# Dilated queries, keys and gates as pairs of 7 block products instead of direct matmuls woven with the attention

## The chip, the cores and the metric

The kernel runs on one core of a Trainium2 chip. TensorE (PE) multiplies, VectorE (DVE), ScalarE (ACT) and GpSimd (POOL) do the elementwise work, SyncE (SP) issues most DMAs and ACT some. Each engine takes its instructions from a queue of its own in order; semaphores between engines make one wait for another. The metric is device microseconds of one execution, median of the runs.

## The reference

The reference is one encoder block over 1024 tokens of width 1024, float32, with three token mixers side by side. Cut to what matters here:

```python
h = rms_norm(x, g_pre)
a_qkv, bq, bk, bv, mq, ga, gb, gm, mg = split(h @ w_in)
aq, ak = rope(a_qkv[:, :, 0], pos), rope(a_qkv[:, :, 1], pos)   # 3 dilations x 8 heads x 64
for gi, (window, dil) in enumerate(((128, 1), (512, 4), (2048, 16))):
    o_g, lse_g = dilated_window_attention(aq[gi], ak[gi], av[gi], window, dil)
oa = sum(softmax(lse over the dilations) * o_g)                 # "combine"
ob, om = grouped_query_attention(...), memory_attention(...)
ya = (oa * silu(ga)) @ w_br_a                                   # likewise yb, ym: "branch products"
merged = sum(sigmoid(mg + b_merge)[i] * (ya, yb, ym)[i])        # 3 x 1024 merge gates
out = x + rms_norm(merged @ w_out, g_post)
```

## The kernel before

All activations are kept transposed, channels in partitions and 1024 tokens along the row. To keep float32 accuracy every operand is split into a high and a low part (`split`, L104: ACT copies the high part, DVE subtracts it, L105/L106), and a product takes three matmuls: high by high, high by low, low by high. `hh[k]`, `hl[k]` are the parts of the normalised input, eight blocks of 128 channels. A *unit* is 128 output channels for all tokens: 8 blocks x 3 matmuls x 2 halves of 512 tokens = 48 matmuls of 512 columns (`dense`, L143, L145, L147).

The stages in order are: norm and loads; memory attention; grouped-query attention; the values of the dilated attention; the dilated attention; the merge gates; the branch products; the output projection.

The values and the merge gates are computed in pairs of units by a scheme of seven block products: a pair is a 2 x 2 block matrix (weights halved along channels, tokens halved), the sums of blocks are prepared beforehand (weight sums `sf` on POOL, L1430, and their splits `ch`; sums of token blocks T1 to T4, stored in memory `tsd` early in the kernel), and seven products of 12 matmuls take the place of eight: 84 matmuls, not 96. Sums of the products give the outputs. Before, each product of a gate pair has a PSUM bank of its own, and DVE rebuilds the outputs (L1453, tiles `v`, `y`, `w`; ACT copies the first product into `p1`, L1467).

The dilated attention has 12 items (4 pairs of heads x 3 dilations). An item needs its query unit and key unit, both turned by rope from PSUM (`rope_half`: four DVE multiplications of 32 partitions and one of 128, L1044/L1045, then a POOL addition, L1051), and then for 8 tiles T of 128 queries: scores on PE (`scores`, L1118), a masked reduction on DVE (`soft`, L1130), exponentials on ACT with their sum (L1133 to L1138; where the two heads' window has to be turned about, in two instructions), transpositions of the probabilities on PE into one of two PSUM banks (`trans`, L1155/L1164), ACT's copy of them out (`app`, L1167), the product with the values (`pv`, L1181), and the sums turned by a transposition (`stats`, L1200). `combine` weighs the three dilations of a pair of heads through a round trip to memory.

The order of PE is written out: `weave` (L174) takes pieces of attention and matmuls of the dense units by turns, by a table of costs, so that matmuls stand between the attention's pieces. 28 units are woven into the attention (24 query and key units, 4 gate units, `add_a`, `add_gate`), two items ahead of the item that reads them. After them come eleven pairs for 22 merge gates (`prod`, `evac`, `slot`), with the last `combine` spread among them; then 24 branch products (`y_unit`, 24 matmuls each, L125, with `y_evac`), then the output. In the value, gate and branch stages the order of ACT, DVE, POOL and SP is written out too; in the attention a scheduler sets it.

```python
                if T == 7:
                    out.append(joined(it["pv"][0], nxt and nxt["scores"][0]))
```
is how a piece of one item and one of the next are put together in the plan of pieces.

## Time and profile before

| | us |
|---|---|
| median of three runs (1447.92 to 1448.38) | 1448.18 |
| span of the profiled execution | 1446.0 |
| PE busy | 1418.7 |
| values, on PE until | 580.35 |
| dilated attention with 28 units, until | 1008.0 |
| eleven gate pairs, until | 1222.07 |
| branch products, until | 1352.63 |
| output projection and end | 93.4 |

Times in rows are microseconds from the start of the span unless a column says ns. A group's row gives line, engine, operation, what it writes and reads, shapes and count, then its busy time, the mean ns of one, and the idle time of the engine just before. Matmuls overlap in the pipeline, so the mean of one is longer than the step from one to the next; the step is read from the chain. The granted TensorE clock was 1.000 over the span.

### The profile page before, as it was taken

Reading aid. Unit: us, or ns where it says so; the run is one execution under the profiler, and the core shown is the slowest. Engines: PE = TensorE matmul, PEld = TensorE weight load, DVE = VectorE, ACT = ScalarE, POOL = GpSimd, SP = SyncE. Lnnn points to the kernel's source line nnn. Section 1 sums busy time; section 2 is a strip of 40 time slices with the busy share of each in tenths; the row PEclk is TensorE's granted clock in tenths of the full one; section 3 lists DMA queues with packets and bytes.
Section 4 is the critical chain, followed back from the end, with each engine's and each line's share of the span. In section 5 each row is a group of like instructions: output and inputs, shape, how many; then the busy total and the mean of one; then the engine's idle time right before and its main releaser. Section 6 shows DMA issues by size and latency. Waiting matters only on the chain.

```text
span 1446.0 us, 20923 instructions
## 1 busy us (share of the span) xinstructions
PE 1418.7 (98%) x7548; PEld 1138.1 (79%) x7548; DVE 986.5 (68%) x1740; ACT 641.7 (44%) x1442; POOL 500.5 (35%) x382
## 2 busy tenths in 40 slices
PE   7999999999999999999999999999999999999998
PEld 7899986565666888878778777778877888888887
DVE  7765468776762267786696786863878787559643
ACT  6544365665654253254445445554443444223231
POOL 1415504666664420232232241321323331044322
PEclk9999999999999999999999999999999999999999
DMA  6332022232111675411132142343444443757122
GB/s 239 103 117 74 16 66 91 81 106 74 55 52 60 242 228 175 137 48 44 49 98 78 45 103 62 92 129 88 140 147 138 175 175 113 286 206 282 44 88 102
DMA packets 99448, 168.05 MB, mean 116 GB/s; under 512 B 21968, under 2 KB 51856, under 8 KB 99344
## 3 DMA queue, kind: packets, MB, share of 16 engines
q1 hardware_dynamic: 80192, 148.76, 31.7%
q10 hardware_dynamic: 19152, 17.96, 3.7%
q8 instruction: 59, 0.97, 0.3%
q14 instruction: 45, 0.37, 0.1%
HBM read 124.38 MB, written 42.30 MB: 115 GB/s over the span
## 4 chain that ended last, share of the span: by engine, by line
PE 78%; DVE 6%; ACT 5%; issue 4%; POOL 3%; DMA 3%; ACTq 0%; SPq 0%; POOLq 0%; DVEq 0%
PE d L145 9%; PE sc L125 9%; PE d L147 9%; PE d L143 9%; PE s L125 8%; PE s L962 6%; PE sc L1703 5%; PE ov L751 3%; PE tr L1181 2%; PE d L962 2%; PE tr L717 2%; PE s L735 2%; PE s L736 2%; PE s L1118 2%; PE d L535 2%
## 5 line engine op out<-in xcount | busy, mean ns | idle before, releaser
L143 PE MATMUL d<-hh,wh 128*128 128x512 f32 x672 | 269.7, 401 | 1.7 <-DVE fth L222 1.7
L147 PE MATMUL d<-hh,wl 128*128 128x512 f32 x672 | 268.0, 399 | 0.0
L145 PE MATMUL d<-hl,wh 128*128 128x512 f32 x672 | 267.9, 399 | 0.0
L105 ACT ACTIVATE wh<-wr 128x1024 fp32r<-128x1024 f32 (+1 forms) x79 | 72.2, 917 | 209.9 <-PE d L145 114.9
L143 PEld LDWEIGHTS d<-hh,wh 128*128 128x128 f32 x672 | 126.6, 188 | 31.3 <-issue 4.9
L145 PEld LDWEIGHTS d<-hl,wh 128*128 128x128 f32 x672 | 126.6, 188 | 31.1 <-issue 8.4
L742 POOL TENSOR_TENSOR bl<-bl,bp 128x512 f32<-128x512 f32 x96 | 131.5, 1369 | 53.4 <-ACT bp L738 48.0
L147 PEld LDWEIGHTS d<-hh,wl 128*128 128x128 f32 x672 | 126.5, 188 | 28.5 <-issue 4.8
L125 PE MATMUL sc<-hh,wh 128*128 128x512 f32 x384 | 118.4, 389 | 0.0
L1051 POOL TENSOR_TENSOR aq<-t1a,t2a 128x512 f32<-128x512 f32 x24 | 45.3, 1889 | 170.5 <-DVE t1a L1045 156.3
L718 DVE TENSOR_REDUCE bn<-tr 128x1 f32<-128x512 f32 x128 | 85.9, 685 | 17.2 <-PE tr L717 15.9
L738 ACT ACTIVATE bp<-s 128x512 f32<-128x512 f32 x128 | 75.8, 595 | 46.6 <-PE s L736 44.9
L106 DVE TENSOR_TENSOR wl<-wr,wh 128x1024 fp32r<-128x1024 f32 x53 | 74.0, 1398 | 30.7 <-ACT wh L105 30.2
L1051 POOL TENSOR_TENSOR ak<-t1a,t2a 128x512 f32<-128x512 f32 x24 | 55.5, 2311 | 106.9 <-DVE t1a L1044 106.9
L1044 DVE TENSOR_TENSOR t2a<-d,tab 32x512 f32<-32x512 f32 x96 | 66.0, 687 | 37.7 <-PE d L147 36.4
L1430 POOL TENSOR_TENSOR sf<-wr 128x512 f32<-128x512 f32 x22 | 30.4, 1400 | 162.3 <-DVE ch L106 74.7
L125 PEld LDWEIGHTS sc<-hh,wh 128*128 128x128 f32 x384 | 72.1, 188 | 15.1
L1045 DVE SCALAR_TENSOR_TENSOR t2a<-d,tab 32x512 f32<-32x512 f32 x96 | 66.0, 687 | 25.9 <-PE d L147 24.4
L1634 POOL TENSOR_TENSOR acc<-acc,th 128x1024 f32<-128x1024 f32 x15 | 40.9, 2729 | 110.6 <-DVE th L1633 110.6
L125 PE MATMUL sc<-hl,wh 128*128 128x512 f32 x192 | 74.7, 389 | 0.0
L1138 ACT ACTIVATE pra<-pra,sts 128x128 f32<-128x128 f32 (+2 forms) x152 | 66.4, 439 | 13.6 <-DVE sts L1130 13.6
L1130 DVE CUSTOM_DVE_ANT_0 pra<-s,mask 128x192 f32<-128x192 f32 (+2 forms) x192 | 55.7, 347 | 15.8 <-PE s L1118 14.9
(375 smaller groups left out, 3434.7 us busy)
## 6 DMA issues: line engine op xcount, KB each, us to landing
wr<-in_wu SPq DMA_DIRECT2D x64, 512.0 KB
th<-thd SPq DMA_DIRECT2D x24, 512.0 KB
thd<-rs ACTq DMA_DIRECT2D x44, 256.0 KB
g2d<-fth SPq DMA_DIRECT2D x24, 256.0 KB
vdr<-vr ACTq DMA_DIRECT2D x24, 256.0 KB
wgt<-wgd SPq DMA_DIRECT2D x24, 256.0 KB
ot<-od SPq DMA_DIRECT2D x12, 512.0 KB
wr<-in_wbr SPq DMA_DIRECT2D x24, 256.0 KB
```

Source lines behind the costliest of these rows:

```text
L105: A.activation(dst_h, src, AF.Copy)
L106: V.tensor_tensor(dst_l, src, dst_h.bitcast(F32), op=OP.subtract)
L125: PE.matmul(out_ps, a, b, start=i == 0, stop=i == n - 1)
L143: PE.matmul(dst, wh[:, k, :], hh[k][:, t], start=k == 0, stop=False)
L145: PE.matmul(dst, wh[:, k, :], hl[k][:, t], start=False, stop=False)
L147: PE.matmul(dst, wl[:, k, :], hh[k][:, t], start=False, stop=k == 7)
L718: fp["last"] = V.tensor_reduce(st[i]["n"][:, j, c:c + 1], s, axis=AX.X, op=OP.min)
L738: A.activation(pp, s, AF.Exp, scale=-1.0)
L742: G.tensor_tensor(lsum[i % 2], lsum[i % 2], pp, op=OP.add)
L962: PE.matmul(now[j], a, b, start=k == 0 and q == 0, stop=k == end and q == 2)
L1051: G.tensor_tensor(half_of(o, half, g), classes(t1, g), classes(t2, g), op=OP.add)
L1703: PE.matmul(parts[h], *terms[h][j], start=j == 0, stop=j == 23)
```

## The change

The 24 query and key units and the 4 dilated gates leave the attention. They become 14 more pairs of seven block products, ahead of the eleven merge-gate pairs: 25 pairs in one stage right after the values, in the same six PSUM banks and with the same layout of token sums. All pairs sum their products in PSUM: products 1, 3, 5 and 7 follow each other into bank a, 4 and 6 into bank b, 2 into bank c. Partial sums are copied out of bank a by ACT as they stand (`p1`, `v_`, `y_`; L1174, L1178), and DVE makes one addition for three of the four outputs (L1132), into a tile `rs` in SBUF. Rope then runs from `rs`, with the rows of weights and tables reordered so that two multiplications of 64 partitions take the place of four of 32. The turned queries and keys are stored to memory (`qkd`) and loaded again by `qk_load`, two items ahead.

T2 and T3 are loaded anew at the start of the stage and split there; T1 and T4 stay from the values. The gate products of the memory branch are made during the values (`operand_m`).

The attention follows the block products. It is woven with 12 of the 24 branch products (`Y_WOVEN`): those of the memory branch and half of the grouped-query branch; their operands are loaded and split there (`b_load`, `b_split`, `a_load`, `a_split` at places listed in `HOOK`). The scores of turned windows are written to PSUM in turned order, by two matmuls, so that each exponential is one instruction; the copies of transpositions of odd tiles are made by DVE. The last `combine` follows the attention, then four branch products, then the eight of the dilated branch. The attention, branch and output stages leave the order of ACT, DVE, POOL and SP to the scheduler. `dynamic_dma_scratch_size=1024` makes a buffer smaller that this kernel doesn't use.

```diff
+    rest = [j for i in (2, 1, 0) for j in range(8 * i, 8 * i + 8) if j not in FILL_B]
+    seq = [(p_, g) for p_ in range(4) for g in range(3)]
+    pairs = [("qk", (p_ * 6 + g * 2, p_ * 6 + g * 2 + 1), (p_, g)) for p_, g in seq]
+    pairs += [("g", (U_G + a[1], U_G + b[1]), (a[1], b[1])) for a, b in zip(GATES_A[::2], GATES_A[1::2])]
+    pairs += [("m", (U_M + a, U_M + b), (a, b)) for a, b in zip(rest[::2], rest[1::2])]
+    NQ, last = len(seq), len(pairs) - 1
+    BL = {n: {} for n in range(len(pairs))}
+
...
+    def prod(n, x):
+        an, bn = PRODUCT[x]
+        dst = bank_for(n, x)
+        ah, al = [v.rearrange("p (k f) -> p k f", k=4) for v in BL[n][an]]
+        terms = [t for k in range(4) for t in (
+            (ah[:, k], TB[bn][k][0]), (ah[:, k], TB[bn][k][1]), (al[:, k], TB[bn][k][0]))]
+        opens = x in "142" or (x == "7" and n == last)
+        closes = x in "276" or (x == "5" and n == last)
+        for i, (a, b) in enumerate(terms):
+            PE.matmul(dst, a, b, start=opens and i == 0, stop=closes and i == 11, skip_group_check=True)
+
...
+    def out_qk(n, u, t, x, z):
+        p_, g = pairs[n][2]
+        first = (n, u) not in O_
+        if first:
+            O_[n, u] = rp.tile([P, S], F32, name="o", bufs=3)
+        o = O_[n, u]
+        r = rs_()
+        if z is not None:
+            V.tensor_tensor(r, x, z, op=OP.add)
+            x = r
+        t2 = rp.tile([P, 512], F32, name="t2", bufs=2)
+        cos, sin = tab[0][:, half[t]], tab[1][:, half[t]]
+
+        def mult(out, a, b):
+            if u:
+                return V.tensor_tensor(out, a, b, op=OP.mult)
+            return V.scalar_tensor_tensor(out, a, -0.125, b, op0=OP.mult, op1=OP.mult)
+
+        for i, j in ((slice(0, 64), slice(64, 128)), (slice(64, 128), slice(0, 64))):
+            mult(t2[i], x[j], sin[j])
+        mult(r, x, cos)
+        G.tensor_tensor(half_of(o, t, g), classes(r, g), classes(t2, g), op=OP.add)
+        if not first:
+            nc.sync.dma_start(qkd[p_, g, u], o)
+
...
+    def evac(n, x):
+        a, b, c = [banks_of.get((n, i)) for i in "abc"]
+        if x in "13":
+            A.activation(p1 if x == "1" else v_, a, AF.Copy)
+        elif x == "2":
+            return output(n, 0, 0, c, p1)
+        elif x == "5":
+            A.activation(y_, a, AF.Copy)
+            outs = output(n, 1, 1, b, y_)
+            if n == last:
+                outs += output(n, 1, 0, banks_of[n, "d"], y_)
+            return outs
+        elif x == "7" and n < last:
+            return output(n, 1, 0, a)
+        elif x == "6":
+            return output(n, 0, 1, b, v_)
+        return []
+
...
+    def qk_load(n):
+        p_, g = seq[n]
+        d = OPS[p_, g] = {}
+        for u, nm in enumerate("qk"):
+            d[nm] = aq.tile([P, S], F32, name=f"a{nm}", bufs=2)
+            for h in range(2):
+                for f in range(2):
+                    i, j = h * 64 + f * 32, f * 64 + h * 32
+                    nc.sync.dma_start(d[nm][i:i + 32], qkd[p_, g, u, j:j + 32])
+
...
+        if n == 0 and x == "1":
+            for k in range(4):
+                split_block("T3", k)
...
+    order = []
+    for n in range(len(pairs)):
+        if n:
+            order += [(n, "1"), (n - 1, "7"), (n - 1, "6")]
+        order += [(n, x) for x in ("12345" if n == 0 else "4325" if n < last else "437526")]
+
...
+            for h in half:
+                s = psd()
+                terms = []
+                for k in range(4):
+                    gh, gl = [x[k + 4 * (i == 1)][:, h] for x in (hh, hl)]
+                    terms += [(wh[:, k], gh), (wh[:, k], gl), (wl[:, k], gh)]
+                for q, (a, b) in enumerate(terms):
+                    PE.matmul(s, a, b, start=q == 0, stop=q == 11)
+                    yield 216
+                if i == 2:
+                    V.scalar_tensor_tensor(accs[f][:, h], th[:, h], 1.0, s, op0=OP.add, op1=OP.mult)
+                else:
+                    V.scalar_tensor_tensor(th[:, h], th[:, h], 1.0, s, op0=OP.add, op1=OP.mult)
+                    G.tensor_tensor(accs[f][:, h], accs[f][:, h], th[:, h], op=OP.add)
...
-        mask = aa.tile([P, 384], F32, name="mask")
+        mask = aa.tile([P, 512], F32, name="mask")
         nc.sync.dma_start(mask, msk)
...
-            for a in range(4):
-                i, j = slice(32 * a, 32 * a + 32), slice(32 * (a ^ 1), 32 * (a ^ 1) + 32)
-                mult(t2[i], p[j], sin[j])
...
+                        cuts = [(0, lo, hi)]
+                        if turned(T, h):
+                            c = lo + blocks_of(T)[0][2]
+                            cuts = [(0, c, hi), (hi - c, lo, c)]
+                        for o, a, c in cuts:
+                            PE.matmul(raws[T][h][:, o:o + c - a], qa[hs, T * 128:T * 128 + 128], ka[hs, a:c],
+                                      start=True, stop=True)
 
...
+                if T % 2:
+                    V.tensor_copy(pp[:, :k], tp[:, :k])
+                else:
+                    A.activation(pp[:, :k], tp[:, :k], AF.Copy)
...
+        HOOK = {(0, 5): lambda: [b_load(k) for k in (0, 1)], (1, 4): lambda: [b_split(k) for k in (0, 1)],
+                (1, 5): lambda: [b_load(k) for k in (2, 3)], (2, 4): lambda: [b_split(k) for k in (2, 3)],
+                (9, 1): lambda: a_load(0), (9, 5): lambda: a_split(0),
+                (10, 1): lambda: a_load(1), (10, 5): lambda: a_split(1),
+                (11, 1): lambda: a_load(2), (11, 5): lambda: a_split(2)}
+
...
+        weave(Y_WOVEN, run(pieces), sum(c for _, c in pieces), 1.0)
+        GG[0, 3] = [aa.tile([P, S], F32, name="ot", bufs=2)]
+        nc.sync.dma_start(GG[0, 3][0], g2d[0, 3])
+        for f in combine(3, [OG.pop((3, x)) for x in range(3)]):
+            f()
+        weave(16 - Y_WOVEN)
...
-        elif nm == "S2":
-            add(v, ps_, p1)
-        elif nm == "S3":
-            add(y, ps_, v)
-        elif nm == "S4":
-            add(w, ps_, v)
```

Three places in the order of instructions. The first is ACT where the gate pairs (before) or all pairs (after) begin. `sf` is a weight sum, `ch` its split, `sp` the copy of the first product; `aq` and `ak` are buffers that hold token sums there. Before:

```order
L105 ACTIVATE ch<-sf_9952 128x512
L1467 ACTIVATE sp_9957<-s_9975 128x512
L105 ACTIVATE ch<-sf_9953 128x512
L105 ACTIVATE ch<-wr 128x512
L105 ACTIVATE ch<-sf_9954 128x512
L105 ACTIVATE aq<-aq 128x512
L105 ACTIVATE ak<-ak 128x512
```

After, with `T_5856` to `T_5867` the four tiles each of T2 and T3:

```order
L105 ACTIVATE ch<-sf_5847 128x512
L105 ACTIVATE T_5856<-T_5856 128x512
L105 ACTIVATE T_5857<-T_5857 128x512
L105 ACTIVATE T_5858<-T_5858 128x512
L105 ACTIVATE T_5859<-T_5859 128x512
L105 ACTIVATE ch<-sf_5848 128x512
L105 ACTIVATE ch<-sf_5849 128x512
L105 ACTIVATE T_5864<-T_5864 128x512
L105 ACTIVATE T_5865<-T_5865 128x512
L105 ACTIVATE T_5866<-T_5866 128x512
L105 ACTIVATE T_5867<-T_5867 128x512
L1174 ACTIVATE sp_5851<-s_5891 128x512
```

The copy of the first product stood behind one split and now stands behind eleven.

The second is SP at the start of the attention. `mask` is the score mask, `avs` and `avp` are values of an item, `ot` the grouped-query result, `wl<-thd` a stored merge gate, `wr<-in_wbr` branch weights. Before:

```order
L874 DMA sl<-tsd 128x512 x3
L940 DMA od<-vot 128x512
L874 DMA sl<-tsd 128x512
L114 DMA wr<-in_wu 128x1024 x2
L1018 DMA mask<-in_msk 128x384
L1085 DMA avs<-vdr 128x7x128
L1093 DMA avp<-vdr 64x2x64 x2
L114 DMA wr<-in_wu 128x1024 x4
L1096 DMA avp<-vdr 64x4x64 x2
```

After:

```order
L1265 DMA wr<-in_wbr 128x512
L1267 DMA wl<-thd 128x1024
L1265 DMA wr<-in_wbr 128x512
L1267 DMA wl<-thd 128x1024
L1265 DMA wr<-in_wbr 128x512 x2
L1355 DMA avs<-vdr 128x7x128
L1363 DMA avp<-vdr 64x2x64 x2
L1510 DMA ot<-od 128x1024 x2
L1331 DMA mask<-in_msk 128x512
L1199 DMA aq<-qkd 32x1024 x4
L1199 DMA ak<-qkd 32x1024 x4
```

The mask was issued during the values, and is now issued behind the loads of the first branch products, the values of the first item and two result tiles.

The third is PE in the middle of the attention, `d` being the dense unit or branch product and `tr` a transposition or a product with the values. Before:

```order
L1164 MATMUL tr<-cs,pra 128x128 x4
L143 MATMUL d<-hh_88,wh 128x512
L145 MATMUL d<-hl_96,wh 128x512
L147 MATMUL d<-hh_88,wl 128x512
L143 MATMUL d<-hh_89,wh 128x512
L145 MATMUL d<-hl_97,wh 128x512
L1155 MATMUL tr<-cs,pra 128x128 x3
L147 MATMUL d<-hh_89,wl 128x512
L143 MATMUL d<-hh_90,wh 128x512
L145 MATMUL d<-hl_98,wh 128x512
L1200 MATMUL tr<-cs,sts 32x128
L147 MATMUL d<-hh_90,wl 128x512
```

After:

```order
L1282 MATMUL d<-hh_90,wh 128x512
L1435 MATMUL tr<-cs,pra 128x128 x2
L1282 MATMUL d<-hh_91,wh 128x512
L1435 MATMUL tr<-cs,pra 128x128 x2
L1282 MATMUL d<-hl_99,wh 128x512
L1435 MATMUL tr<-cs,pra 128x128 x2
L1282 MATMUL d<-hh_91,wh 128x512
L1435 MATMUL tr<-cs,pra 128x128 x2
L1282 MATMUL d<-hh_92,wh 128x512
L1282 MATMUL d<-hl_100,wh 128x512
L1282 MATMUL d<-hh_92,wh 128x512
L1456 MATMUL tr<-app,avs 64x128 x8
```

Between two pieces of attention there stood three to five dense matmuls here, and now one to three.

649 lines of the change are left out of this document (281 added, 368 removed).

## The prediction

> **What bounds the kernel now.** I read the page's totals, then the busy times by stage, then the chain and the waits of single engines.
>
> The page's head says that TensorE (PE) is the bound nearly everywhere:
> ```profile
> span 1446.0 us, 20923 instructions
> PE 1418.7 (98%) x7548; PEld 1138.1 (79%) x7548; DVE 986.5 (68%) x1740; ACT 641.7 (44%) x1442; POOL 500.5 (35%) x382
> ```
> Busy time by stage: window and its length, then busy us and instruction count of PE, weight loads, DVE, ACT, POOL, then granted clock, DMA share, GB/s. The rows are the values, the dilated attention (two rows), the eleven gate pairs (two rows) and the branch products:
> ```profile
> 461.00:580.00 119.00, 119.00 (x527) 98.53 (x526) 65.66 (x93) 44.01 (x74) 26.74 (x18) 1.00 0.63 207
> 580.00:616.00 36.00, 36.00 (x160) 29.81 (x159) 27.08 (x39) 8.26 (x10) 9.12 (x5) 1.00 0.45 136
> 616.00:1008.00 392.00, 385.90 (x2504) 309.99 (x2502) 282.23 (x692) 193.80 (x638) 106.01 (x49) 1.00 0.28 76
> 1008.00:1118.00 110.00, 108.12 (x470) 87.23 (x468) 86.18 (x108) 45.81 (x72) 41.90 (x26) 1.00 0.42 137
> 1118.00:1222.00 104.00, 103.88 (x457) 85.72 (x458) 84.38 (x107) 44.11 (x68) 31.97 (x20) 1.00 0.43 150
> 1222.00:1353.00 131.00, 131.00 (x580) 108.47 (x579) 95.09 (x77) 33.16 (x50) 40.93 (x15) 1.00 0.63 231
> ```
> PE hardly idles in any stage at full clock. So the time is a count of PE instructions plus PE's waits, and I forecast it as that. The chain in order of time (start, us, engine, line, count) gives the step:
> ```profile
> 569.47 10.88 PE s L962 x48
> ...
> 1222.07 130.56 PE sc L125 x576
> 1352.63 66.58 PE sc L1703 x294
> ```
> 130.56/576 = 0.2267 us per 512-column matmul. The values end on PE at 580.35, the attention at 1008.0, the gate pairs at 1222.07, the branch products at 1352.63; 93.4 us follow.
>
> **The floor: the new count, with no wait.** A unit has 48 such matmuls (10.88 us), a pair of two units 96, as 7 block products 84 (19.04 us). 14 pairs save 14 x 12 = 168 matmuls, 38.1 us. The attention stage was 427.7 us; its 28 units were 28 x 10.88 = 304.7, its idle 6.1 (392.00 less 385.90), so its own PE work is 116.9. The turned scores add 40 small matmuls; I take 2 us (estimate; at most 40 steps, 9). After:
>
> 580.3 + 25 x 19.04 (476.0) + attention 118.9 with 12 branch products of 24 matmuls (5.44 each, 65.3) + the other 12 (65.3) + 93.4 = 1399.2 us. That is 46.8 under 1446.0: 38.1 fewer matmuls, 6.1 idle in the attention and 4.6 waits in the gate pairs (214.1 less 11 x 19.04), less 2. So up to 46.8 us of new waits leave the time unchanged. I go through the places.
>
> **Start of the block products.** ACT copies the first product out of its bank (L1174 of the new code), and the third product sums into that bank. Ahead of the copy, ACT has 11 splits of weights and token sums; ahead of those the last value outputs.
> ```profile
> 576.26 2.01 ACT L105 ACTIVATE wh<-wr 128x1024 fp32r<-128x1024 f32 x2 [0.44 <-ACT vr L900]
> ...
> 588.01 0.72 ACT L900 ACTIVATE vr<-vr,rcol 128x512 f32<-128x512 f32 x1 [0.72 <-ACT vr L900]
> 588.76 0.37 ACTq L901 DMA_DIRECT2D vdr<-vr  x1
> ...
> 1010.86 0.63 ACT L105 ACTIVATE ch<-sf 128x512 fp32r<-128x512 f32 x1 [1.45 <-POOL sf L1430]
> 1011.39 0.58 ACT L1467 ACTIVATE sp<-s 128x512 f32<-128x512 f32 x1
> ```
> Before, ACT ends the value outputs at 589.1, which nobody waited for. One of the two weight splits among them is gone (1.0), so 588.1. Twelve instructions at 0.53 (1010.86 to 1011.39) end at 594.5; PE is done with two products at 580.35 + 24 x 0.2267 = 585.8. I take 9 us of wait, 4 to 11 (less where the outputs come earlier).
>
> **A query/key pair on DVE and POOL.** The copies of partial sums cost ACT 0.58 three times per pair. Each has one product (2.7 us) of cover or more before the bank is written again, with at most one split of 1.05 ahead of it on ACT; without that cover each would cost PE about 1 us. The v, y and w additions on DVE go. What is new is that rope now works from SBUF: three of four outputs are first added into `rs` (L1132), then multiplied (L1139/1140, three instructions in place of five).
> ```profile
> 581.50 1.21 DVE L106 TENSOR_TENSOR wl<-wr,wh 128x1024 fp32r<-128x1024 f32 x1
> ...
> 1119.42 0.69 DVE L1459 TENSOR_TENSOR rs<-rs,rb 128x512 f32<-128x512 f32 x1
> 1120.03 0.69 DVE L106 TENSOR_TENSOR ch<-sf,ch 128x512 fp32r<-128x512 f32 x1
> ...
> 1122.37 2.05 DVE L106 TENSOR_TENSOR wl<-wr,wh 128x1024 fp32r<-128x1024 f32 x1 [1.05 <-ACT wh L105]
> ...
> 1124.95 1.18 DVE L106 TENSOR_TENSOR ch<-sf,ch 128x512 fp32r<-128x512 f32 x1
> ...
> 624.75 2.14 POOL L1051 TENSOR_TENSOR ak<-t1a,t2a 128x512 f32<-128x512 f32 x1 [5.01 <-DVE t1a L1044]
> ...
> 672.88 1.29 POOL L1051 TENSOR_TENSOR aq<-t1a,t2a 128x512 f32<-128x512 f32 x1 [7.80 <-DVE t1a L1045]
> ...
> 1120.80 2.54 POOL L1430 TENSOR_TENSOR sf<-wr 128x512 f32<-128x512 f32 x2 [8.63 <-DVE ch L106]
> 1123.31 2.27 POOL L1430 TENSOR_TENSOR sf<-sf,wr 128x512 f32<-128x512 f32 x1
> 1125.66 1.62 POOL L1430 TENSOR_TENSOR sf<-wr,sf 128x512 f32<-128x512 f32 x1
> ```
> Instructions of 512 columns stand 0.61 apart on DVE (1119.42 to 1120.03). Per pair it has three additions, twelve multiplications and five splits of that size and one of 1.21: 13.4 us. POOL has four sums at 1.29 and four rope additions, 1.29 for the first dilation, about 2.1 for the others: 10.3 or 13.6. Each alone fits 19.04. They slow each other where DVE reads two SBUF operands: the split of 1.21 took 2.05 beside POOL, the one of 0.61 took 1.18, and POOL's four sums 6.4 in place of 5.2. There 7.3 us of work (5.2 on POOL, one split and two parts of one on DVE, 2.1) were done in 6.4. 2.8 of it was unopposed (1120.80 to 1122.37, and two additions from PSUM of 0.6), so 4.5 in 3.6: together they go at 1.25 times one. 9.8 of DVE's 13.4 us is of that kind (all splits, 4.3, and the nine multiplications of `rs`). With 3.6 of it free, a pair of the slow dilations needs 3.6 + (9.8 + 10.0)/1.25 = 19.4 us, one of the first 16.8: 18.5 on average against 19.04. I take 3 us over 12 pairs, 0 to 9.
>
> The Trainium skill ("SBUF — State Buffer", section "SBUF: two separate sides") says that this port pair is an exclusive lock, held for a whole instruction by a DVE operation with two SBUF inputs or by GpSimd, while the other blocks. This case's overlap of 1.25 is near that rule but not it; what the rule would make of the time is the third rival below.
>
> **Start of the attention.** Before, the mask was loaded long ahead. Now SP issues it behind two branch-weight loads (the last waits for DVE's split of the second branch weight, at about the end of the last product), three value loads and two loads of the grouped-query result. ACT's splits of that result stand ahead of its first exponentials.
> ```profile
> 735.36 4.38 SPq L1299 DMA_DIRECT2D wgt<-wgd  x6
> 739.78 1.25 SPq L1096 DMA_DIRECT2D avp<-vdr  x2
> ...
> 755.54 0.34 SPq L1088 DMA_DIRECT2D avs<-vdr  x1
> ...
> 759.01 0.36 SPq L114 DMA_DIRECT2D wr<-in_wu  x1
> ...
> 744.60 5.42 DVE L1329 TENSOR_TENSOR og<-og,wgt 128x1024 f32<-128x1024 f32 x2
> ...
> L105 ACT ACTIVATE hh<-ot 128x1024 fp32r<-128x1024 f32 x8 | 8.4, 1046 | 0.0
> ```
> Seven issues of 0.34 to 0.63 are about 3 us. A landing is at most 4.9 (the last `wgt` issue ends at 739.74, the weighing that reads it starts at 744.60); I take half. So the mask lands about 5.3 us after the end of the last product, two splits of 1.05 end at 6.8, four exponentials (0.45 each) at 8.7. PE has 17 instructions to do meanwhile, 3.2 us. With 1 us before (the last product's weight split stands on DVE behind four output instructions) and 1 at the second transposition: 7.5, 2 to 12.
>
> **In the attention.** Between attention pieces PE has mostly one to three branch matmuls where it had three to six. Two PSUM banks take all transpositions, and each bank waits for ACT's copy of it.
> ```profile
> L1138 ACT ACTIVATION_READ_ACCUMULATOR pra<-pra,sts 128x1 f32 x152 | 28.7, 189 | 0.0
> ...
> L1138 ACT ACTIVATE pra<-pra,sts 128x192 f32<-128x192 f32 x40 | 17.7, 443 | 0.0
> ...
> L1329 DVE TENSOR_TENSOR og<-og,wgt 128x1024 f32<-128x1024 f32 x12 | 29.4, 2473 | 0.0
> ```
> and PE's waits there (us in total, times, longest):
> ```profile
> PE tr L1200 <- ACT app L1167: 3.7, 6, 0.9
> PE tr L1155 <- ACT app L1167: 2.4, 5, 1.6
> ```
> A half-item is about 8 us of PE work; ACT's copy of a transposition stands behind up to five exponentials (2.2 us). The waits above are 0.5 to 0.6 each. Two per item, 12 items: 13 us; none at best, and at worst 0.45 (one exponential) at each of 96 steps, 43. The 22 long DVE instructions (twelve of the combines, 2 to 2.5 us; seven splits; three gate products) delay the score reductions behind them: 4, 0 to 15. Exponentials in one instruction instead of two (40 fewer) and half of the copies moved to DVE are in ACT's favour, and priced in the count.
>
> **The last combine.** It lay beneath the gate pairs; now only four branch products (21.8) and the first 2 us of the fifth cover it.
> ```profile
> 727.27 0.17 DVE L1309 TENSOR_TENSOR cmn<-cpt 128x16 f32<-128x16 f32 x1
> ...
> 733.45 1.26 SPq L1322 DMA_DIRECT2D wgd<-ceg  x2
> ```
> The weights take 6.2 (727.27 to 733.45), their issues 1.3 and 4.4, two landings 5, and three weighings of 2 to 2.5 with their additions behind them about 8; a product and a split of 1.05 and 1.2 follow. That is 27 against 23.8. Wait 3.5, 0 to 10.
>
> Moved at no price: the memory branch's gate products (four DVE instructions, 6 MB of DMA) go under the values, where DVE has 65.66 of 119.00; its cost if that cover fails is 5. The query/key tiles go through memory: 24 stores of 512 KB from SP, and 96 loads of a quarter of that, issued an item or two ahead, 8 per item at 0.36 or 2.9 of some 17 us of SP; if SP is late by that, it is 3 per item, inside the chain rival. Branch-product evacuation is half as wide and twice as often, under 5.44 us each.
>
> **Sum.** 9 + 3 + 7.5 + 13 + 4 + 3.5 = 40 us of waits on 1399.2: 1439.2. The three runs' median, 1448.18, is 2.2 above the span of the profiled execution; with the same, **1441.5 us**, 0.46% faster.
>
> **Rivals.** *All of it arrives*: PE never waits beyond the start of the products and half of the others; waits 20, time 1421. For it: ACT and DVE were at 49% and 72% there. Against: so little PE work stands between pieces. *The attention follows its chain of reductions, exponentials and copies*: PE waits 0.45 at each of 96 steps, 43 in place of 13, time 1471; slower by over 0.2% begins at 49.7 us of waits in all, which is 22.7 in the steady attention, 1.9 per item. For it: a step has 1.9 us of PE work (184.2/96), and in that time two reductions on DVE, two exponentials (0.9) and half a copy on ACT must follow each other, in a fixed order and with two banks between. Against: the reductions of a step run two steps ahead of its transpositions, so a single delay under some 2 us costs nothing. *DVE and POOL never work together*: a pair needs 9.8 + 12.5 = 22.3, 3.2 over 19.04 and 38 over twelve pairs in place of 3, time 1477; the measured 1.25 speaks against it. (By the Trainium skill's lock this is what would happen, its page named above.)
>
> **How the numbers follow.** Forecast with waits of 28 to 52: 0.52 (faster 0.37, same 0.09, slower 0.06). All arrives: 0.15, faster. Chain: 0.27 (slower 0.25, same 0.02). Lock: 0.06 (slower 0.05, same 0.01). Within 0.2%, 2.9 us, a measurement of this kernel can hardly tell a change. Faster 0.52, same 0.12, slower 0.36. The range leaves out the lowest and highest tenth: 1418 to 1468; the forecast's own is 1430 to 1454.
>
> **What would show it.** PE should show 14 x 12 fewer matmuls; a wait of about 9 us in the first query/key pair for ACT's copy, and about 5.5 just after the last pair for the exponentials; the pairs 19.0 to 19.4 us apart; PE waits in the attention of 13 to 20 us, on transpositions after ACT copies; under 5 us at the fifth unwoven branch product. An attention stage over 216 us with its start makes me wrong; so do pairs over 20 us.

## The result: 9.1% slower

The changed kernel takes 1579.95 us (median of four runs, 1578.83 to 1581.66), the kernel before 1448.28 us beside it (four runs, 1447.92 to 1448.80). The ratio is 1.091, with a 95% interval of 1.0894 to 1.0925. The forecast was 1441.5 us, and its range ended at 1468.

The page's head of the kernel after, span and busy times of the engines:

```profile
span 1578.4 us, 21012 instructions
PE 1429.6 (91%) x7460; PEld 1129.2 (72%) x7460; DVE 1022.0 (65%) x1746; ACT 665.1 (42%) x1426; POOL 602.6 (38%) x455
```

PE lost 88 instructions (168 fewer large matmuls, 80 more small ones), yet its busy time rose by 11 us, and it idles for 149 us in place of 27. The busy time by stage of the kernel after (columns as in the prediction; the rows are the values, the start of the block products, the query/key pairs, the gate pairs, and two stretches of attention and branch products):

```profile
461.00:586.83 125.83, 122.43 (x530) 100.00 (x529) 73.13 (x98) 43.59 (x74) 31.25 (x21) 0.99 0.73 246
586.83:605.49 18.66, 5.60 (x25) 4.32 (x23) 9.90 (x16) 11.69 (x20) 0.00 (x0) 0.77 0.89 279
605.49:889.17 283.68, 254.65 (x1056) 198.36 (x1056) 271.05 (x259) 71.02 (x116) 195.56 (x99) 0.99 0.26 91
889.17:1125.10 235.93, 234.27 (x1020) 192.62 (x1021) 131.75 (x177) 105.09 (x165) 61.12 (x46) 0.99 0.39 128
1125.10:1334.00 208.90, 154.27 (x1253) 118.86 (x1253) 100.48 (x379) 105.64 (x365) 12.93 (x7) 0.89 0.54 144
1334.00:1484.70 150.70, 122.68 (x722) 95.97 (x719) 91.61 (x196) 55.53 (x154) 55.63 (x33) 0.92 0.53 165
```

Against the floor of 1399.2 us (counted matmuls at 0.2267 us each), the span of 1578.4 is 179 us over. By stage:

| stage | counted | measured | over |
|---|---|---|---|
| until PE ends the values | 580.35 | 586.83 | 6.5 |
| start of the block products (25 matmuls) | 5.7 | 18.66 | 13.0 |
| query/key pairs (1056 matmuls) | 239.4 | 283.68 | 44.3 |
| gate pairs (1020 matmuls) | 231.2 | 235.93 | 4.7 |
| attention with twelve branch products, until its last value product ends at 1403.0 | 184.2 | 277.9 | 93.7 |
| the other branch products, with the last combine | 65.3 | 81.7 | 16.4 |
| output and end | 93.4 | 93.7 | 0.3 |

The three large ones are taken one at a time.

**Query/key pairs.** In the third row DVE is busy for 271.05 of 283.68 us and PE idles for 29. 1056 matmuls are 12.57 pairs, so a pair takes 22.6 us; PE's pattern of waits repeats every 69 us, which is three pairs, one for each dilation. A few rows of the timeline of DVE and POOL in this stage of the kernel after (start, us, engine, line; `o<-rs,t` is rope's addition on POOL, `ch<-sf,ch` a weight split and `rs<-s,sp` an addition from PSUM on DVE):

```profile
705.49 2.54 POOL L1145 TENSOR_TENSOR o<-rs,t 128x512 f32<-128x512 f32 x1 [0.63 <-DVE rs L1140]
705.94 0.68 DVE L1132 TENSOR_TENSOR rs<-s,sp 128x512 f32<-128x512 f32 x1
...
710.93 3.23 DVE L106 TENSOR_TENSOR ch<-sf,ch 128x512 fp32r<-128x512 f32 x2
711.09 2.51 POOL L1145 TENSOR_TENSOR o<-rs,t 128x512 f32<-128x512 f32 x1 [1.35 <-DVE rs L1139]
```

The two splits would take 1.3 us alone. POOL's addition ends at 713.60 and the second split at 714.16, 0.56 later, which is the time of one split: it was done entirely behind the addition. The addition from PSUM, in the midst of another POOL addition, took 0.68, its usual time. So in these rows DVE stands still until the POOL instruction ends where it reads two SBUF operands, and not where one of them is in PSUM. The page "SBUF — State Buffer" of the Trainium skill (section "SBUF: two separate sides") calls it an exclusive lock held for the whole instruction; these rows agree with it.

**Start.** The chain of the kernel after, in order of time, between the values and the second product's sum:

```profile
588.53 4.83 DMA vdr<-vr
...
594.96 5.92 DMA vdr<-vr
...
601.26 3.04 DMA T<-tsd
...
604.32 0.63 ACT T L105
604.95 0.49 ACT sp L1174
605.45 0.04 issue
605.49 0.80 PE s L1117
```

PE waits from 592.43 to 605.49, 13.1 us, for the copy of the first product. ACT reaches that copy late not for the length of its eleven splits: the last of them wait for T tiles, whose loads SP could issue only when stores of value outputs had landed (5.92 us for the last store, 3.04 for the load behind it).

**Attention.** PE's waits between 1125 and 1485 in the kernel after (engine, line, what it waited for: us in total, times, longest):

```profile
PE d L1282 <- ACT wh L105: 16.1, 3, 8.4
PE d L1282 <- DVE wl L1287: 12.6, 3, 8.2
PE tr L1426 <- ACT og L1464: 9.6, 1, 9.6
PE tr L1426 <- ACT pra L1409: 9.5, 2, 8.5
PE tr L1469 <- ACT app L1441: 7.8, 9, 1.3
PE tr L1435 <- ACT app L1441: 5.6, 9, 1.6
```

The first four rows hold five long waits of 7.0 to 9.6 us. The one of 8.5 is the mask at the start. What the other four wait for is a split, a gate tile or a copy, but what is behind these is a load. SP's own queue before the second of the five, in which PE waits from 1204.45 to 1212.81 for a branch weight:

```profile
1198.91 2.39 SPq L1199 DMA_DIRECT2D aq<-qkd  x4
1201.34 3.62 SPq L1199 DMA_DIRECT2D ak<-qkd  x4
1207.57 1.26 SPq L1614 DMA_DIRECT2D wgd<-ceg  x2
1208.87 0.60 SPq L1265 DMA_DIRECT2D wr<-in_wbr  x1
```

The weight's load was issued at 1208.87, 4.4 us after PE had begun to wait for it: eight query and key loads, and a store of the combine whose data was not ready, stood ahead of it in the same queue.

PE idles for 72.0 of the attention's 277.9 us and is busy for 205.9, which is 21.7 more than the 184.2 counted. Added up over windows of 1 us (PE's busy time, times what the granted clock lacks of 1), about 15 of these 21.7 come from the clock, which was 0.90 over the attention and 0.50 behind the long waits. Most of the rest is the scores, which keep PE busy for 43.7 us (464 matmuls) where they took 37.0 before (384); 2 us of that were counted.

### The profile page after: what moved, and what is told of

The parts are those of the page before. It is cut to its first block, busy times and chain, and to the rows that moved or that the text cites. A ratio compares the mean times of both kernels' runs of the same rounds, so it can differ in the third digit from the quotient of the medians.

```text
span 1578.4 us, 21012 instructions
## 1 busy us (share of the span) xinstructions
PE 1429.6 (91%) x7460; PEld 1129.2 (72%) x7460; DVE 1022.0 (65%) x1746; ACT 665.1 (42%) x1426; POOL 602.6 (38%) x455
## 4 chain that ended last, share of the span: by engine, by line
PE 53%; DVE 20%; DMA 10%; issue 6%; ACT 5%; POOL 3%; SPq 2%; ACTq 0%; DVEq 0%; POOLq 0%
PE s L1117 17%; PE sc L1702 4%; DVE ch L106 4%; PE d L1282 4%; PE ov L752 3%; DVE t L1139 3%; DVE t L1140 3%; PE d L145 3%; PE d L147 3%; PE d L143 3%; PE tr L1456 2%; ACT pra L1409 2%; DMA vdr<-vr 2%; PE tr L718 2%; PE s L736 2%
## 5 line engine op out<-in xcount | busy, mean ns | idle before, releaser
L1117 PE MATMUL s<-T,ch 128*128 128x512 f32 x900 | 217.5, 395 | 14.6 <-ACT sp L1174 14.4
L1117 PEld LDWEIGHTS s<-T,ch 128*128 128x128 f32 x900 | 170.0, 190 | 55.5 <-ACT sp L1174 17.9
L1282 PE MATMUL d<-hh,wh 128*128 128x512 f32 x384 | 143.2, 433 | 33.1 <-ACT wh L105 16.1
L1117 PE MATMUL s<-hh,ch 128*128 128x512 f32 x392 | 131.2, 402 | 27.1 <-ACT sp L1178 16.6
L1145 POOL TENSOR_TENSOR o<-rs,t 128x512 f32<-128x512 f32 x48 | 112.9, 2351 | 110.7 <-DVE rs L1140 60.6
L106 DVE TENSOR_TENSOR ch<-sf,ch 128x512 fp32r<-128x512 f32 x100 | 109.6, 1107 | 39.6 <-ACT ch L105 39.5
L1117 PEld LDWEIGHTS s<-hh,ch 128*128 128x128 f32 x392 | 75.1, 192 | 51.5 <-ACT sp L1178 21.2
L1409 ACT ACTIVATE pra<-pra,sts 128x192 f32<-128x192 f32 (+2 forms) x192 | 84.0, 439 | 29.9 <-DVE sts L1408 29.8
L105 ACT ACTIVATE ch<-sf 128x512 fp32r<-128x512 f32 x100 | 61.3, 626 | 83.3 <-POOL sf L1080 82.7
L147 PE MATMUL d<-hh,wl 128*128 128x512 f32 x224 | 89.2, 398 | 0.0
L145 PE MATMUL d<-hl,wh 128*128 128x512 f32 x224 | 89.1, 398 | 0.0
L1174 ACT ACTIVATE sp<-s 128x512 f32<-128x512 f32 x50 | 29.7, 594 | 140.6 <-DVE rs L1132 94.8
L1282 PE MATMUL d<-hl,wh 128*128 128x512 f32 x192 | 80.9, 421 | 1.1 <-DVE hl L106 1.1
```

The source lines that it names most:

```text
L105: A.activation(dst_h, src, AF.Copy)
L106: V.tensor_tensor(dst_l, src, dst_h.bitcast(F32), op=OP.subtract)
L145: PE.matmul(dst, wh[:, k, :], hl[k][:, t], start=False, stop=False)
L147: PE.matmul(dst, wl[:, k, :], hh[k][:, t], start=False, stop=k == 7)
L1117: PE.matmul(dst, a, b, start=opens and i == 0, stop=closes and i == 11, skip_group_check=True)
L1145: G.tensor_tensor(half_of(o, t, g), classes(r, g), classes(t2, g), op=OP.add)
```

## Experiments

Single runs beside the kernel before (1448.0 to 1449.1 on those chips) unless an interval is given; the four runs of the changed kernel itself lie within 3 us, so a difference of that size says nothing.

**1. Rope's addition on DVE instead of POOL.** It puts more work on the busier engine, and takes these additions off POOL.

```diff
-        G.tensor_tensor(half_of(o, t, g), classes(r, g), classes(t2, g), op=OP.add)
+        V.tensor_tensor(half_of(o, t, g), classes(r, g), classes(t2, g), op=OP.add)
```

> The rope addition of a query/key pair moves from POOL to DVE; the result is the same. In the changed kernel the twelve query/key pairs take 283.7 us (605.49 to 889.17) where their matmuls need 242. Theory A (DVE with two SBUF operands and POOL exclude each other): the sum of what excludes falls from 9.8 on DVE and 12.5 on POOL to 9.8 + 2.4 and 5.2, 17.4 us under a pair's 19.04, so the pairs take about 243 us and the time falls by some 38 us to about 1540. Theory B (DVE's own work, busy 98% there, is the bound): DVE gets 2.4 us more per pair or, with strided writes, up to 8, so the pairs take 310 to 350 us and the time rises to 1605 or more.

Measured: 1543.47 us, 36.5 less; the query/key pairs run from 605.55 to 855.02 on PE, 249.5 us in place of 283.7. The groups of DVE in that stage, first of the kernel after, with POOL's addition (busy us, mean ns of one):

```profile
L106 DVE TENSOR_TENSOR ch<-sf,ch 128x512 fp32r<-128x512 f32 x50 | 73.5, 1490 | 2.3 <-ACT ch L105 2.1
L1140 DVE SCALAR_TENSOR_TENSOR t<-rs,tab 64x512 f32<-64x512 f32 x48 | 56.9, 1186 | 2.8
...
L1132 DVE TENSOR_TENSOR rs<-s,sp 128x512 f32<-128x512 f32 x36 | 24.5, 680 | 2.4 <-ACT sp L1178 1.7 <-PE s L1117 0.7
...
L1145 POOL TENSOR_TENSOR o<-rs,t 128x512 f32<-128x512 f32 x48 | 112.9, 2351 | 110.7 <-DVE rs L1140 60.6 <-DVE rs L1139 50.1
```

and of this experiment:

```profile
L1145 DVE TENSOR_TENSOR o<-rs,t 128x512 f32<-128x512 f32 x48 | 47.2, 983 | 1.6
L1140 DVE SCALAR_TENSOR_TENSOR t<-rs,tab 64x512 f32<-64x512 f32 x48 | 40.9, 852 | 1.2
L106 DVE TENSOR_TENSOR ch<-sf,ch 128x512 fp32r<-128x512 f32 x50 | 33.2, 683 | 1.3 <-ACT ch L105 1.3
L1132 DVE TENSOR_TENSOR rs<-s,sp 128x512 f32<-128x512 f32 x36 | 24.6, 685 | 2.6 <-ACT sp L1178 1.8 <-PE s L1117 0.8
```

A split falls from 1490 to 683 ns, fifty of them from 73.5 to 33.2 us, while the addition from PSUM keeps its duration (680, 685). DVE does 48 instructions more in less time.

**2. The multiplications read the PSUM bank.** As many instructions on DVE and POOL as in the changed kernel, but the three outputs that were multiplied from SBUF are now multiplied from PSUM too. What this leaves out is the partial sum.

```diff
             V.tensor_tensor(r, x, z, op=OP.add)
-            x = r
```

> The multiplications of rope read the PSUM bank and not the summed tile in SBUF, so DVE and POOL issue the same instructions but nine of DVE's per pair have one SBUF operand less. (The partial sum is left out of queries and keys.) Theory A: what excludes is 4.3 on DVE and 12.5 on POOL, 16.8 us under 19.04; the pairs take about 243 us, the time about 1540. Theory B (DVE's own count, or the chain from bank to copy to addition): the instructions and their order are the same, so 283.7 and 1578 stay.

Measured: 1537.72 us, 42.2 less. A hundred microseconds amid the pairs, of the kernel after:

```profile
700.00:800.00 100.00, 86.74 (x362) 66.43 (x361) 98.03 (x92) 26.18 (x43) 71.83 (x36) 1.00 0.29 100
```

and of this experiment:

```profile
700.00:800.00 100.00, 100.00 (x441) 82.37 (x440) 93.83 (x111) 28.88 (x47) 77.33 (x42) 1.00 0.30 106
```

PE no longer waits there. So it is neither the number of DVE's instructions nor POOL's load, but that both of DVE's operands lie in SBUF while POOL works there.

**3. The first copy ahead of the T3 splits.**

```diff
-        if n == 0 and x == "1":
+        if n == 0 and x == "2":
             for k in range(4):
                 split_block("T3", k)
```

> The four splits of T3 stand behind ACT's copy of the first product. Theory A (the copy is late because ACT has eleven splits ahead of it): four splits and their loads less, so the wait of 13.1 us at the third product falls to about 9, and the fifth product, which needs T3, still doesn't wait: 4 us less in all and under 1 us less of half clock. Theory B (the loads of T2 and T3, issued on SP behind the value stores, set it): the wait moves to the fifth product or stays, and the time stays within 1 us.

Measured: 1582.85 us, 2.9 more, within the scatter; the wait shrinks to 10.6 us (594.22 to 604.81), but the stage of block products takes 538.4 us as before (538.3). The loads of T set the start, not ACT's order.

**4. PE kept busy through the start.** 56 matmuls that nobody reads, in the place of the wait.

```diff
         prod(n, nm)
+        if (n, nm) == (0, "2"):
+            dj, (ja, jb) = psd(), BL[0]["A11"]
+            for q in range(56):
+                PE.matmul(dj, ja[:, 0:128], TB["B11"][0][0], start=q == 0, stop=q == 55)
```

> 56 matmuls whose result nobody reads fill the 13.1 us wait of PE at the start of the pairs; nothing else changes. Theory A (PE's clock is halved after an idle of some us and takes about 5 us of work to come back, as windows of the trace show with a granted clock of 0.50 from 604 to 610): the clock stays 1.00 there, the 108 matmuls after the wait step at 0.227 and not 0.252, and 2.7 us are saved in the first pair. Theory B (the slow step there is waits for operands): no change in the step.

After the wait in the changed kernel, PE's granted clock (the tenth column) is half for some 5 us:

```profile
606.00:608.00 2.00, 2.00 (x6) 1.52 (x5) 1.97 (x3) 0.48 (x1) 0.00 (x0) 0.50 0.36 39
608.00:610.00 2.00, 2.00 (x6) 1.52 (x6) 1.95 (x4) 0.00 (x0) 0.49 (x1) 0.50 0.87 295
610.00:612.00 2.00, 2.00 (x9) 1.62 (x8) 0.03 (x1) 1.17 (x2) 2.00 (x2) 0.89 0.49 199
612.00:614.00 2.00, 2.00 (x10) 1.60 (x9) 1.59 (x2) 1.01 (x2) 1.92 (x2) 1.00 0.00 0
```

With the extra matmuls it stays whole, in the same place of this experiment:

```profile
606.00:612.00 6.00, 6.00 (x27) 4.80 (x26) 5.51 (x8) 2.65 (x5) 1.87 (x2) 1.00 0.51 175
```

The stage is 2.3 us shorter (536.0), which is about what 5 us at half clock cost; the total, 1575.99, is 4.0 less, little more than the scatter of runs. So the clock row shows the effect, and the size of it rests on one run.

**5. The mask loaded during the gate pairs**, as a tile of the pool that holds the query/key tiles.

```diff
             aqp, aq = pool("aqk", "right")
+            mask = aq.tile([P, 512], F32, name="mask")
+            nc.sync.dma_start(mask, msk)
             qk_load(0)
...
-        mask = aa.tile([P, 512], F32, name="mask")
-        nc.sync.dma_start(mask, msk)
```

> The mask is loaded during the gate pairs, as early as the first query tile. Theory A (the late mask is what PE's 8.5 us of waiting at the start of the attention ends on): the reductions start as soon as the scores are there, and the wait falls to what two splits of the grouped-query result ahead of the exponentials on ACT leave, 3 to 6 us. Theory B (those splits, whose tiles are loaded just ahead of the mask, end it): the wait stays at 7 to 8.5.

Measured: 1571.05 us, 8.9 less. In place of the wait of 8.5 us, the longest there is now 1.7.

**6. Quarters stored rather than loaded.** SP issues 96 stores where it had 24, in the stage of block products, where it is idle, and 24 loads in the attention where it had 96.

```diff
-            nc.sync.dma_start(qkd[p_, g, u], o)
+            for h in range(2):
+                for f in range(2):
+                    i, j = h * 64 + f * 32, f * 64 + h * 32
+                    nc.sync.dma_start(qkd[p_, g, u, i:i + 32], o[j:j + 32])
...
-            for h in range(2):
-                for f in range(2):
-                    i, j = h * 64 + f * 32, f * 64 + h * 32
-                    nc.sync.dma_start(d[nm][i:i + 32], qkd[p_, g, u, j:j + 32])
+            nc.sync.dma_start(d[nm], qkd[p_, g, u])
```

> The queries and keys are stored in four parts (96 stores in the pairs' stage, where SP is idle for most of the time) and loaded by one DMA each (24 and not 96 in the attention); the result is the same. Theory A (SP's queue is what PE waits for in the attention: the four waits of 7 to 9.6 us there end on a branch weight, a gate or a copy that stands behind late issues of SP): 72 issues of 0.45 us less, 32 us of SP, and most of these 33 us go, with 8 to 10 us of half clock behind them: 25 to 40 us less in all. Theory B (the chain of exponentials and copies sets the attention): less than 8 us.

Measured: 1547.26 us, 32.7 less; attention and branch products take 327.8 us in place of 359.6. PE's waits between 1123 and 1452 of this run:

```profile
PE tr L1426 <- ACT pra L1409: 9.7, 2, 8.8
PE tr L1456 <- DMA avs<-vdr: 9.7, 3, 5.2
...
PE d L1282 <- DVE wl L1287: 4.2, 2, 3.1
```

The mask's wait stands; the four others of 7 to 9.6 us are gone, and the longest that remains for a load is 5.2. The loads themselves change as well, one of 128 partitions in place of four of 32, and how much of the 32.7 is due to that and not to SP's queue was not separated.

**7. Sixteen branch products woven in place of twelve.**

```diff
-Y_WOVEN = 12
+Y_WOVEN = 16
```

> 16 branch products and not 12 are woven with the attention; none is left beneath the last combine. Theory A (PE waits in the attention anyway): the four more fit into its waits, so the attention grows by less than half of their 21.8 us, and what is lost is the combine's cover: about 27 us less 2 uncovered in place of 4 to 8. Sum about 0 to +10 us. Theory B (the attention is bound by PE's work): it grows by 21.8, and the combine is uncovered besides: +20 to +25.

Measured: 1594.78 us, 14.8 more, between the two expectations. The attention is 20.6 us longer (298.5), nearly the 21.8 of the four products, and PE idles there as long as before (70.4 us, 72.0 in the changed kernel); what follows it is some 6 us shorter. PE's waits from 1123 to 1500:

```profile
PE d L1282 <- ACT wh L105: 30.3, 3, 13.1
PE d L1282 <- ACT hh L105: 26.3, 1, 26.3
```

The last combine, which had four branch products for cover, has none, and PE waits 26.3 us for its result. That is the size of the whole combine, the 27 us of the forecast.

**8. Branch tiles loaded a step further ahead**, with a third set of tiles `yr`, `yt`, `yh` for every third product, and the preparation called for two steps ahead:

```diff
             prepare(n)
             prepare(n + 1)
+            if YP:
+                prepare(n + 2)
...
+            if YP and Y_STEPS.index((i, f)) % 3 == 2:
+                raw = YP[0].tile([P, 512], F32, name="yr")
+                c["th"] = YP[0].tile([P, S], F32, name="yt")
+                t = YP[0].tile([P, 1024], R, name="yh")
```

> A third set of tiles for branch weights, their split and the stored gate, and each is loaded two branch products ahead and not one; the result is the same. Theory A (late loads): the long waits of PE on branch weights and gates (8.4, 7.0 and 8.2 us, and 7.8 between the unwoven products) go, 25 us and about 8 of half clock. Theory B (SP is busy or held in its queue for more than a branch product's time whatever stands in it): the loads are as late as before, and under 8 us are saved.

Measured: 1576.47 us, 3.5 less, about the scatter. The waits of 16.1 and 12.6 us became 6.0 and 18.3, of which one is 16.5. The long waits moved and did not go, as the second expectation had it; what holds these loads up stays open.

**9. The edits of experiments 1, 5 and 6 together.**

> Three edits together, the result being the same: rope additions on DVE, mask loaded early, queries and keys stored in four parts and loaded by one DMA. Alone they took 36.5, 8.9 and 32.7 us off. If they sit in different places they add up: about 1502 us, still 3.7% over the kernel before; if the late loads are partly the same wait, 1505 to 1515.

Measured: 1507.53 us (four runs, 1503.71 to 1510.46), ratio to the kernel before 1.0406 (1.0384 to 1.0428). That is 72.4 less, where the three alone add up to 78.1; the four runs lie too far apart to tell the two. Block products from 589.1 to 1093.4, attention from 1093.8 to 1331.2, all branch products by 1412.7. No wait over 4.2 us is left in the attention, yet it takes 237.4 us where 184.2 were counted, and PE's granted clock is still half for some 29 us of it.

**10. On that, 4 of the 24 matmuls of each woven branch product**, 240 fewer, 54 us of PE's counted work.

```diff
-                    PE.matmul(s, a, b, start=q == 0, stop=q == 11)
+                    if Y_STEPS.index((i, f)) >= Y_WOVEN or q in (0, 11):
+                        PE.matmul(s, a, b, start=q == 0, stop=q == 11)
```

> The three edits of the run before, and of the 24 matmuls of each branch product that is woven with the attention only the first and last of each half are issued (4 of 24; the others are left out of the result). 12 x 20 matmuls of 0.2267 are 54.4 us less PE work between the attention's pieces. Theory A (the stage is a count of PE work plus few waits, as the prediction had it): it gets about 50 us shorter. Theory B (the attention has a pace of its own, set by reductions, exponentials, copies and loads): the matmuls ran in its waits, and it gets less than 20 us shorter.

Measured: 1513.94 us, 6.4 more. The attention lasts from 1092.3 to 1336.8, 244.5 us, about 20 for an item. So fewer matmuls did not shorten it, though four products more had lengthened it by nearly their whole count (experiment 7). The run does not show that the attention has a pace of its own, because leaving the matmuls out also lowered the clock: it was 0.82 over the attention, where experiment 9 had 0.94. PE idles for 74.2 us there in place of 36.9, and, added up over windows of 1 us, its busy time holds some 37 us that are due to half clock in place of 12.5. The 54 us came back as 37 of waits and 25 of slower clock, and how far the clock lengthened the waits is open.

**11. Without the memory branch's gate products** (on the changed kernel):

```diff
-            if at == 0 and 0 <= r < 4:
+            if at == 0 and 0 <= r < 4 and False:
                 operand_m(r, stage)
```

> The changed kernel without the gate products of the memory branch beneath the values (they are left out of the result): eight loads and four stores of 512 KB and four DVE instructions less. In the changed kernel the block products start at 586.8 and not 580.35, with one wait of 3.4 us on DVE behind such a load. Theory A (these transfers slow the values): the start comes back to 580 to 582, and with less traffic the value stores land earlier, so the 13.1 us wait shrinks as well, by 2 to 5; 6 to 11 us less in all. Theory B (the new splits of T1 and T4 beneath the values do it): the start stays at 585 or later.

Measured: 1570.74 us, 9.2 less. The block products begin at 580.6 in place of 586.8, and PE's wait at their start is 11.5 us. The gate products under the values cost 6.2 us ahead of the block products, and some of the start.

**12. All copies of transpositions on DVE** (on experiment 9):

```diff
-                if T % 2:
-                    V.tensor_copy(pp[:, :k], tp[:, :k])
-                else:
-                    A.activation(pp[:, :k], tp[:, :k], AF.Copy)
+                V.tensor_copy(pp[:, :k], tp[:, :k])
```

> The three edits together, and all copies of transpositions on DVE, not half of them on ACT behind its exponentials. In the three edits' trace PE's waits of 21 us in the attention end on ACT's copies and 5 on DVE's. Theory A (each wait is the copy's place in ACT's queue): most of the 21 us go, DVE's own queue gives 5 to 10 back, 10 to 15 us less than 1507. Theory B (a half-item is a chain of scores, reductions, exponentials, transpositions and copies that PE has to wait through whoever copies): the waits move to DVE's copies and the time stays within 5 us.

Measured: 1507.57 us, no change. PE's waits for copies are now for DVE's.

**13. 96 more exponentials that nobody reads** (on experiment 9), 42 us more of ACT by their durations:

```diff
+                    if h == 0:
+                        A.activation(aa.tile([P, 256], F32, name="xj", bufs=1)[:, :n], src, AF.Exp, scale=-1.0, bias=bias)
                     A.activation(src, src, AF.Exp, scale=-1.0, bias=bias, accum_out=sts[:, h, 1, T:T + 1])
```

> The three edits together, and for the first head of each tile one more exponential whose result nobody reads, 96 times 0.44 us: 42 us more on ACT, which is busy for 162 us of the 323 from the first branch product to the last. Theory A (PE waits on the chain through the exponentials): most of it is added to the stage, 25 to 45 us. Theory B (loads, or PE's own count, set the pace and ACT's idle half takes it): under 10 us.

Measured: 1528.27 us, 20.7 more. Half of ACT's added work shows, though ACT is busy for 143.92 of 246 us there (1094 to 1340 in experiment 9). So ACT seems to be on the path for about half of the time. In the trace of experiment 9 it idles, for one, 2.4 us until PE ends a value product (1155.48) and 0.5 us more for the first of the scores behind it. The clock over the attention is lower here too, 0.92 in place of 0.94, so a part of the 20.7 is that.

**14. Scores two tiles at a time** (on experiment 9). In place of four tiles' scores at once behind a value product, two tiles' scores follow the reductions that free their banks. The loads of the item two ahead (`more`) now stand behind the item's last scores:

```diff
-            def scores(b):
-                if b == 0:
+            def scores(c):
+                if c == 0:
...
-                for j in range(4):
-                    T = 4 * b + j
+                for j in range(2):
+                    T = 2 * c + j
...
+                    if T == 0 and pre:
+                        out.append(it["scores"][1])
                     out.append(it["soft"][T])
+                    if T in (2, 4):
+                        out.append(it["scores"][T // 2 + 1])
+                    if T == 4:
+                        out.append((more, 0.0))
...
+                    if T == 6 and nxt:
+                        out.append(nxt["scores"][0])
...
-                    out.append(joined(pre and pre["pv"][1], it and it["scores"][1]))
+                    out.append(joined(pre and pre["pv"][1]))
```

> On the three mendings together (1507.5 us, attention with its branch products 1093.8 to 1412.7), the scores of an item are issued two tiles at a time, each pair of tiles right after the reductions of an earlier pair, in place of four tiles at once behind the product with the values; the same instructions otherwise. Theory A (what is left in the attention is an alternation: PE stands while ACT works off the exponentials of four tiles, and ACT stands about 3.4 us per four tiles while PE does the value product and the next four scores): PE's waits for copies and ACT's idle both shrink, up to 24 x 3 us, so 1440 to 1490. Theory B (a chain of reduction, exponential, transposition, copy within each tile, or the two transposition banks, sets the pace whatever the order of the scores): within 10 us of 1507, with as many waits for copies of transpositions (app) as before.

Measured: 1494.42 us (four runs, 1492.41 to 1495.60), ratio to the kernel before 1.032 (1.0302 to 1.0337); 13.1 less than experiment 9, between the two expectations. PE's waits in the attention, first of experiment 9:

```profile
PE tr L1469 <- ACT app L1441: 9.4, 10, 1.4
PE tr L1426 <- ACT app L1441: 6.2, 4, 3.9
...
PE tr L1435 <- ACT app L1441: 5.4, 8, 1.6
```

and of this run:

```profile
PE tr L1469 <- ACT app L1441: 4.4, 9, 1.6
...
PE tr L1435 <- ACT app L1441: 1.6, 2, 1.3
...
PE tr L1426 <- ACT app L1441: 1.1, 1, 1.1
```

The waits for ACT's copies fall from 21.0 to 7.1 us, so the alternation of scores and exponentials was real; undoing it was worth 13 us in all. The rest of the excess isn't waiting of that kind. The same 226 us of both (1094 to 1320), first of experiment 9:

```profile
1094.00:1320.00 226.00, 191.76 (x1628) 151.04 (x1628) 132.90 (x490) 134.71 (x468) 28.15 (x14) 0.94 0.56 168
```

and of this run:

```profile
1094.00:1320.00 226.00, 205.58 (x1704) 150.55 (x1703) 143.28 (x516) 145.10 (x492) 27.19 (x15) 0.99 0.58 175
```

The granted clock rises from 0.94 to 0.99 with it. So the gain may be of both, shorter waits and the clock that no longer falls behind them; they were not separated.

305 of these 1704 matmuls are dense ones, 69.1 us at 0.2267. That leaves 136 us of PE's busy time for the attention's own pieces, where the forecast had 118.9, and 20 us of idle time in short waits. The scores are the larger part of the 17 us between: 464 matmuls keep PE busy for 47.1 us, where 384 took 37.0 before and the forecast added 2 for the difference. For the rest, that the latency of short pieces was hidden before behind dense neighbours is my reading and was not measured apart (busy PE is modelled).

This is the fastest version that was run, and still 46 us slower than the kernel before. Over the floor it has about 8 us ahead of the block products, 31 in their stage, 37 in the attention (221.2 for 184.2) and 16 in the last branch products. Weaving gate pairs instead of branch products into the attention was not tried.

## Why the prediction was wrong, step by step

- **The count**: right for the large matmuls; the turned scores add 80 small ones, where 40 were counted at 2 us, and the scores keep PE busy for 6.7 us more than before. Output and gate pairs take about what was counted (93.7 for 93.4, 235.9 for 231.2).
- **"A query/key pair on DVE and POOL", 3 us (0 to 9)**: measured 44, of which the lock rival had said 38. The step that failed is "together they go at 1.25 times one". It was read from one stretch of 6.4 us in the gate pairs, by setting durations against each other that already contain the waiting. The ends of the four rows shown there say more: DVE's split of 2.05 ends at 1124.42, POOL's next sum at 1125.58, DVE's next split at 1126.13, POOL's last sum at 1127.28. The steps of 1.16, 0.55 and 1.15 are each about the time of one such instruction alone (1.29 and 0.61), so they ran one after another, with some 0.1 of overlap at each change. The 22.3 us per pair of the rival given 0.06 is what came (22.6), and experiments 1 and 2 show it is the cause. The Trainium skill's rule, weighed in the forecast and set aside, held.
- **"Start of the block products", 9 us (4 to 11)**: measured 13.1. The path was another: not ACT's eleven splits, but loads behind stores of the values (experiment 3). The price of half a clock behind the wait was left out, 2.3 us here (experiment 4).
- **Memory gate products under the values, at no price, "5 if that cover fails"**: the cover failed: the block products began 6.5 us late, of which experiment 11 takes away 6.2, and 9.2 with what follows.
- **"Start of the attention", 7.5 us (2 to 12)**: 8.5, by the mechanism named; with the mask loaded early the longest wait there is 1.7 (experiment 5).
- **Query/key tiles through memory, at no price, "3 per item" if SP is late**: SP was late; experiment 6 took away 32.7 us, or 2.7 for each of twelve items, some of which may be the shape of the loads. The step that failed is counting SP's 2.9 us of issues against "some 17 us of SP" per item. With the combine's stores, the statistics' and the values' loads in the same queue, in order, and each behind the readiness of its data, the branch weights came late; sharing SP by sums of issue time misses that.
- **"In the attention", 13 us (0 to 43)**: the attention took 277.9 us, past the 216 named as the mark of a wrong forecast. With mask and loads mended it takes 237.4, 53 over the counted 184.2. The chain rival's mechanism is a part of that (experiments 13 and 14): issuing the scores by two tiles takes 16 us off the attention, to 221.2, while the clock rises from 0.94 to 0.99. Of the other 37 about 17 are PE's own pieces, busy for longer than counted, and about 20 short waits. The steps that failed are "a single delay under some 2 us costs nothing", the attention's own work taken from a trace in which dense matmuls stood around it, and a sum at full clock: over the attention of the changed kernel the clock was 0.90, which made PE's busy time some 15 us longer. How the excess splits between chain, clock and pieces is open in part.
- **Long DVE instructions, 4 us**: not seen apart; in the attention of experiment 14 no wait for DVE is over 2 us.
- **"The last combine", 3.5 us (0 to 10)**: 16.4 over the count. The combine's own length, 27 us by the forecast, was right by experiment 7 (26.3); PE's idle time there is 10.7 (82.0 less 71.31 busy between 1403 and 1485), and its clock of 0.94 over those 82 us would make up to another 4.9.
- **The side**: of the rivals that end slower, each was given alone. The lock and the late SP came together with a chain, so the range, made of one mishap at a time, ended 112 us too low.

## What to carry to other kernels

Where DVE reads two SBUF operands beside POOL, add up their times as if they were one engine, as came out here (22.3 us added up for a pair, 22.6 measured), unless a steady stretch of the trace shows otherwise; look at the ends of the instructions there and not at their durations, which contain the waiting; an operand left in PSUM, or the work moved onto DVE itself, frees it. Dense matmuls woven among attention pieces cover short waits, and they keep the granted clock up, so taking them out can cost more than their count saves: ask first what the pieces take, and at which clock, when nothing stands between them. Count a DMA queue by what stands in it in order and by what each entry waits for, not by the sum of its issue times.

## What the runs showed of the hardware

After each wait of 7 us or more in the stages from the block products on, PE's granted clock was 0.50. Where PE then worked steadily it came back to 1.00 some 4 to 5 us after work began: behind the wait that ended at 605.49 it is 0.89 from 610 to 612, behind that of 1212.81 it is 0.50 until 1218 and 1.00 after, behind that of 1329.99 it is half until 1334. The Trainium skill ("TensorE: Matmul & The Clock Gate", Part 1, on the clock gate) gives an idle window of about 3.4 us for the fall to half rate and as much busy time for the return. The fall agrees where PE stopped at 1129.29 and the clock is 0.84 from 1132 to 1133 and 0.50 after; the return took somewhat longer here. It made a long wait cost about 2.3 us more than it lasts (experiment 4), in which the forecast had nothing. Waits that are shorter but close together lower the clock too: in the attention of experiment 9, with none over 4.2 us, it was half for some 29 us, and in that of experiment 10 for some 88.

DVE was held until a POOL instruction ended (0.56 us of split behind an addition that ended at 713.60), yet not when one operand was in PSUM (0.68 amid a POOL addition of 2.54). And rope's strided addition took 983 ns on DVE where it took 2351 on POOL.
